# A pace for the sample's streams of keys and values in a one-core hybrid decoder step, with six stream buffers and 62 slots

## The chip, the cores and the metric

The kernel runs on one core of a Trainium2 chip. The metric is the device time of one execution in microseconds (us); the times stand in the table below.

## What is computed

One inference step of a decoder with a single layer. A prompt of 512 tokens and eight sample tokens (one each for eight requests) go through the same layer: a joint input projection, four heads of a gated linear recurrence and four heads of differential attention, an output projection, cross-attention to a memory of 256 tokens, a SwiGLU network (1024 to 2816 and back) and a last norm. Everything is float32. Each sample request attends to 4096 past tokens, whose keys and values lie in 32 pages of 128 tokens, found by a page table:

```
k_past = cache_k[l][page_table].reshape(dec_b, past_len, DA_HEADS, 2, DA_DH)
v_past = cache_v[l][page_table].reshape(dec_b, past_len, DA_HEADS, DA_DV)
attend_s = functools.partial(diff_attn_sample, k_past=k_past, v_past=v_past)
xs, s_s, k_s, v_s = run_layer(xs, pos_s, state_hgrn[l], attend_s, cache_mem_k[l], cache_mem_v[l], l)
```

A page is 256 KB, so the pages alone are 512 transfers, 134 MB.

## The kernel before

**The prompt.** Its matmuls (accumulators named mm) take float32 weights as a rounded part hi and a remainder lo, and the activations likewise, with three products for each (hi by hi, hi by lo, lo by hi). The weights are walked in one order, the plan: seven column blocks of w_in, then w_mk and w_mv (keys and values of the memory), w_out, w_mq, w_mo, and then w_gate, w_up and w_down by chunks of 512 columns. A plan row is a load of 512 KB (tile raw, three buffers); half a row is one step: ACT rounds it (hi), DVE takes the remainder (lo), and PE runs 12 matmuls with it (6 in the memory's blocks). `done["used"]` counts these steps: w_in is steps 0 to 55, the memory's 56 to 87, w_out, w_mq and w_mo 88 to 135, and the feed-forward network (FFN) starts at step 136. In matmuls of the 3072 in all, step 56 is number 672, step 88 is 864 and step 136 is 1440.

**The sample.** It multiplies the raw weights that the prompt has in SBUF anyway (`follow`: accumulators sacc, sgm, sgu, sdn). Where its data come too late for a chunk of the FFN, it loads those weights once more for itself (`s_ffn_alone` or `gate_alone`, tiles gu, dn, g of 256 KB). Its pages arrive in the stream buffers: `KBUFS` = 8 tiles of two pages (512 KB). `score_keys` (L969) takes four tiles at a time (`LUMP`), a lump of 32 small matmuls into accumulator ks, which a profile shows as 64, two for each; there are 32 such lumps. After the last one follows the sample's softmax (mxt, mxb, zt, cf, wt), then `sum_values` (L1087) with 32 lumps of eight matmuls, accumulator pv. When the values are done, the sample's output projection, its cross-attention (cs, cpv; 32 tiles cache_mem_k and cache_mem_v of 512 KB) and its own copies of w_mq and w_mo come through the same stream buffers (`load_rest`). Other tiles of 128x512 come from a pool of `SLOTS` = 59.

**The order.** The program's text doesn't set it. Each part is a generator, a stream of work; `Weave.run` (L328) builds the program by taking, again and again, the first stream by rank whose next step could start now by the `Clock`, a planner's model of the engines (L231 counts each instruction's cost). Small ranks go first; the prompt has rank 9, keys and values have rank 2 (`KRANK`, `VRANK`), loads of weights 0 and loads of pages 1. All loads are issued by SP, in the order so found, each after its buffer has come free:

```
def add(self, gen, rank, uses=""):
    self.streams.append([rank, 0.0, None, gen, uses])
    self.streams.sort(key=lambda s: s[0])
...
weave.add(score_keys(), KRANK)
...
weave.add(sum_values(), VRANK)
```

Nothing of the planner is in the program that runs; only the order that it found. L295 is the helper through which every instruction is issued, so a profile has that line for all of them, and tiles tell them apart.

Of the kernel before, what the change touches and what calls it, by code (L numbers as in the profile page):

```python
# [25 lines left out]
NB = 8  # L26
# [5 lines left out]
NCH = 8  # L32
# [1 line left out]
LAM_INIT = 0.2  # L34
LEVELS = (16, 8, 4, 2, 1)
BIG = 1e37
SLOTS = 59
SCRATCH = 4
RAW = 3
HILO = 3  # L40
KPG = 2
KBUFS = 8
LUMP = 4
NEAR, FAR = 2, 4
PBATCH = 8
LEAD = 10.0
# [2 lines left out]
KRANK = 2  # L49
# [6 lines left out]
VRANK = 2  # L56
# [64 lines left out]
    return {"consts": packed, "ropep": c["ropep"]}  # L121


TICK, FULL = 3.413, 3060
CHANGE = {
    ("wide", "narrow"): 0.18, ("narrow", "wide"): 0.16, ("exact", "wide"): 0.11, ("exact", "narrow"): 0.18,
    ("narrow", "exact"): 0.06,
# [3 lines left out]
class Clock:  # L131
# [4 lines left out]
    def __init__(self, tc):  # L136
        self.tc = tc
        self.free = dict.fromkeys(("pe", "act", "dve", "pool", "sp", "issue", "dma"), 0.0)
        self.wrote, self.used, self.rings = {}, {}, {}
        self.silu = False  # L140
        self.banks, self.freed, self.noted = {}, deque(), 0
        self.port = {"dve": deque(maxlen=24), "pool": deque(maxlen=24)}
        self.mark, self.columns = 0.0, {}
        self.form = "wide"

    def engine(self, name, nc_engine):
        return Timed(nc_engine, name, self)
# [43 lines left out]
    def _cost(self, e, op, shape, dtypes, n):  # L191
        f32r = F32R in dtypes
        if e == "pe":
            if op == "transpose":
                return 0.00105 * n
            if f32r:
                if shape[0] == 32:
                    return n * 0.000108 + 0.004
                return max(0.03, 0.000432 * n + 0.006)
            if shape[0] in (32, 64):  # L200
                return n * shape[0] / 76800 + 0.003
            return max(0.03, n / 600)
        if e == "act":
            return 0.00083 * n + (0.145 if op == "activation" else 0.04) + (0.03 if f32r else 0)
        if e == "dve":
            if op == "tensor_scalar" and n > 256:
                return 0.00052 * n + 0.067
            return 0.00105 * n + (0.125 if op == "scalar_tensor_tensor" else 0.067)
        return 0.00225 * n

    def shared(self, e, op, outs, srcs):

# [18 lines left out]
    def note(self, e, op, ins):  # L231
        i = ins.ins
        outs = [y.bass_ap for y in i.outs if hasattr(y, "bass_ap")]
        srcs = [y.bass_ap for y in i.ins if hasattr(y, "bass_ap")]
        mine = lambda aps: [a.tensor.name for a in aps if self.tc.is_my_tile(a.tensor)]
        ws, rs = mine(outs), mine(srcs)
        start = self.free[e]
        at = "dma" if op == "dma_start" else e
        for t in ws + rs:
            w, by = self.wrote.get(t, (0.0, ""))  # L240
            if by != at or at == "dma" and t in rs:
                start = max(start, w + self.LATE.get(by, 0.0))
        for t in ws if at != "dma" else ():
            start = max(start, self.used.get(t, 0.0))
        if op == "dma_start":
            start = max(start, self.free["issue"])
            self.free["issue"] = start + 0.56
            self.free[e] = start + (0.56 if e == "sp" else 0.06)
            begin = max(self.free["dma"], start + 1.1)
            a = outs[0] if ws else srcs[0]  # L250
            end = self.free["dma"] = begin + 4 * int(np.prod(a.shape)) / 0.39e6
            done = end + 0.93
            e = "dma"
        else:
            aps = outs + (srcs if e != "pe" else [])
            n = max(int(np.prod(a.shape[1:])) for a in aps)
            holds = self.shared(e, op, outs, srcs)
            if holds:
                for a, b in self.port["pool" if e == "dve" else "dve"]:
                    if a <= start < b:  # L260
                        start = b
            done = end = start + self._cost(e, op, outs[0].shape, [a.dtype for a in outs + srcs], n)
            if e == "pe":
                form = "narrow" if outs[0].shape[0] < P else "wide" if F32R in [a.dtype for a in srcs] else "exact"
                done = end = end + CHANGE.get((self.form, form), 0.0)
                self.form = form
                tick, rows = int(start / TICK), srcs[0].shape[0] / P
                if self.columns.get(tick - 1, 0) < FULL:
                    done = end = end + (end - start)
                self.columns[tick] = self.columns.get(tick, 0) + n * rows * (1 if F32R in [a.dtype for a in srcs] or op == "transpose" else 2)  # L270
            self.free[e] = end
            self.span = (start, end)
            if holds:
                self.port[e].append((start, end))
        for t in ws:
            self.wrote[t] = (done, e)
            self.mark = max(self.mark, done + self.LATE.get(e, 0.0))
        self.noted += 1
        for t in ws + rs:
            self.used[t] = max(self.used.get(t, 0.0), end)  # L280
            if t in self.banks:
                self.banks[t][1] = self.noted
# [19 lines left out]
class Weave:  # L302
# [9 lines left out]

    def add(self, gen, rank, uses=""):
        self.streams.append([rank, 0.0, None, gen, uses])
        self.streams.sort(key=lambda s: s[0])

    def _time(self, s):
        c, t = self.clock, s[1]
# [9 lines left out]
    def run(self):  # L328
        c = self.clock
        while self.streams:  # L330
            now = c.free["pe"]
            best, when = None, 0.0
            for s in self.streams:
                if s[2] is not None:
                    if not s[2]():
                        continue
                    s[2] = None
                t = self._time(s)
                if best is None or t < when:
                    best, when = s, t  # L340
                if t <= now:
                    break
            assert best is not None, "every stream waits"
            c.mark = 0.0
            try:
                y = next(best[3])
            except StopIteration:
                self.streams.remove(best)
                continue
            if y is None:  # L350
                best[1] = c.mark
            elif callable(y):
                best[1], best[2] = 0.0, y
            elif isinstance(y, tuple):
                best[1] = c.ready(y)
            else:
                best[1] = y
# [3 lines left out]
def decode_step(ctx: ExitStack, tc: tile.TileContext, io: dict):  # L361
    clock = Clock(tc)
    weave = Weave(clock)
# [560 lines left out]
    def gather(which, at, dst):  # L924

        for i, t in enumerate(dst, at):
# [5 lines left out]
                clock.free["sp"] += 0.53 + 0.03 * PBATCH  # L932
            page = pages[which][i % PBATCH]
            sync.dma_start(t, ckv[which][bass.ds(page, 1), :, :].rearrange("o p c -> (o p) c"))

    nst = NPG // KPG
    kts, vts, wts = {}, {}, [None] * 4
# [1135 lines left out]
    def sample_query(hs):  # L2073
# [10 lines left out]
        weave.add(load_keys(), 1)  # L2084
        weave.add(load_rest(), 1)
        weave.add(place_queries(), 2)
        weave.add(score_keys(), KRANK)
        yield from at_room()
        acc = att("sk")
        yield from s_gemm(hs, 2560, acc[:, :P], KT, width=P)  # L2090
# [3 lines left out]
        yield from new_scores()  # L2094
        S["sn"] = True
        yield lambda: V_FROM in raws
        weave.add(sum_values(), VRANK)
        weave.add(load_values(), 1)

    def follower():  # L2100
# [490 lines left out]
```

## Time and profile before

| | |
|---|---|
| median of 3 runs | 1152.55 us (1151.62 to 1156.77) |
| the profiled execution | 1153.06 us, span 1151.3 us |
| PE busy | 1089.1 us, 95% of the span |
| DVE, ACT, POOL busy | 545.8, 429.8, 69.0 us |
| moved by DMA | 258.80 MB, mean 225 GB/s |
| mean granted TensorE clock | 0.981 |

PE is TensorE's matmuls, PEld its weight loads, DVE VectorE, ACT ScalarE, POOL GpSimd, SP the engine that issues nearly all DMAs. A matmul's end is modelled in the profile and consecutive ones overlap, so PE's busy time is not its work; that is read from the distance of starts, or from the chain of waits, whose pieces follow each other without overlap. The granted clock 1.00 is 2.4 GHz, half of it 1.2 GHz.

### The profile page before, as it was taken

Reading aid. Unit: us, or ns where it says so; the run is one execution under the profiler, and the core shown is the slowest. Engines: PE = TensorE matmul, PEld = TensorE weight load, DVE = VectorE, ACT = ScalarE, POOL = GpSimd, SP = SyncE. Lnnn points to the kernel's source line nnn. Section 1 sums busy time; section 2 is a strip of 40 time slices with the busy share of each in tenths; the row PEclk is TensorE's granted clock in tenths of the full one; section 3 lists DMA queues with packets and bytes.
Section 4 is the critical chain, followed back from the end, with each engine's and each line's share of the span. In section 5 each row is a group of like instructions: output and inputs, shape, how many; then the busy total and the mean of one; then the engine's idle time right before and its main releaser. Section 6 shows DMA issues by size and latency. Waiting matters only on the chain.

```text
span 1151.3 us, 23340 instructions
## 1 busy us (share of the span) xinstructions
PE 1089.1 (95%) x9035; PEld 787.6 (68%) x9035; DVE 545.8 (47%) x1094; ACT 429.8 (37%) x910; POOL 69.0 (6%) x76
## 2 busy tenths in 40 slices
PE   8999989998998789999999989999999999999997
PEld 6677768776554334556655677778788787777776
DVE  6641667343557554324436355434434345444545
ACT  5411535232734564423325355433222122222333
POOL 0000032120411000000000300000000000000001
PEclk9999989998999899999999999999999999999999
DMA  7999989997997889999989832332232222234002
GB/s 263 376 362 362 369 273 328 364 374 266 302 300 274 306 312 334 364 373 377 385 328 360 330 128 57 91 91 83 83 92 78 88 64 67 64 102 126 20 1 74
DMA packets 139361, 258.80 MB, mean 225 GB/s; under 512 B 14065, under 2 KB 24305, under 8 KB 139250
## 3 DMA queue, kind: packets, MB, share of 16 engines
q1 hardware_dynamic: 138018, 256.20, 64.3%
q8 instruction: 71, 1.16, 0.4%
q10 hardware_dynamic: 1232, 1.11, 0.3%
q14 instruction: 40, 0.33, 0.1%
HBM read 248.38 MB, written 8.88 MB: 223 GB/s over the span
## 4 chain that ended last, share of the span: by engine, by line
PE 74%; DMA 16%; issue 3%; DVE 2%; ACT 2%; SPq 2%; POOL 1%; DVEq 0%; ACTq 0%; POOLq 0%
PE mm L295 53%; DMA cache_v<-cache_v 5%; PE pv L295 4%; PE ks L295 4%; DMA cache_k<-cache_k 3%; PE sdn L295 2%; PE sgu L295 2%; SPq L295 2%; DMA raw<-w_in 2%; DMA cache_mem_k<-cache_mem_k 1%; PE cs L295 1%; PE co L295 1%; PE sgm L295 1%; DMA kv<-vd 1%; ACT pr L295 1%
## 5 line engine op out<-in xcount | busy, mean ns | idle before, releaser
L295 DVE TENSOR_TENSOR lo<-raw,hi 128x512 fp32r<-128x512 f32 (+1 forms) x260 | 177.1, 683 | 428.4 <-ACT hi L295 377.2
L295 PE MATMUL mm<-sh,hi 128*128 128x512 f32 (+1 forms) x832 | 334.2, 402 | 1.4 <-ACT hi L295 1.4
L295 ACT CAST hi<-raw 128x512 fp32r<-128x512 f32 (+1 forms) x260 | 157.1, 607 | 462.0 <-PE mm L295 404.3
L295 PE MATMUL mm<-sl,hi 128*128 128x512 f32 (+1 forms) x832 | 322.7, 388 | 0.6 <-DVE sl L295 0.6
L295 PE MATMUL mm<-sh,lo 128*128 128x512 f32 (+1 forms) x832 | 322.0, 387 | 0.0
L295 PEld LDWEIGHTS mm<-sh,hi 128*128 128x128 f32 x832 | 157.1, 189 | 57.1 <-issue 23.1
L295 PEld LDWEIGHTS mm<-sh,lo 128*128 128x128 f32 x832 | 157.0, 189 | 33.2 <-DVE lo L295 0.9
L295 PEld LDWEIGHTS mm<-sl,hi 128*128 128x128 f32 x832 | 157.4, 189 | 29.4 <-DVE sl L295 1.5
L295 PE MATMUL pv<-cache_v,wt 128*32 128x512 f32 x512 | 81.9, 617 | 7.0 <-DMA cache_v<-cache_v 5.8
L295 PE MATMUL ks<-cache_k,qst 128*32 128x128 f32 x2048 | 66.8, 275 | 4.2 <-issue 2.1
L295 PEld LDWEIGHTS ks<-cache_k,qst 128*32 128x32 f32 x2048 | 55.2, 110 | 17.7 <-issue 8.4
L295 PE MATMUL mm<-hi,sh 128*128 128x512 f32 x128 | 55.8, 436 | 0.0
L295 PEld LDWEIGHTS pv<-cache_v,wt 128*32 128x32 f32 x512 | 18.3, 111 | 53.3 <-DMA cache_v<-cache_v 27.5
L295 PE MATMUL mm<-lo,sh 128*128 128x512 f32 x128 | 50.9, 398 | 0.0
L295 PE MATMUL mm<-hi,sl 128*128 128x512 f32 x128 | 50.8, 397 | 0.0
L295 DVE TENSOR_TENSOR res<-mm,res 128x512 f32<-128x512 f32 (+1 forms) x68 | 41.8, 651 | 6.8 <-PE mm L295 6.7
L295 PEld LDWEIGHTS mm<-hi,sh 128*128 128x128 f32 x128 | 24.7, 193 | 11.8 <-issue 7.8
L295 POOL TENSOR_TENSOR res<-res,par 128x512 f32<-128x512 f32 x2 | 2.3, 1144 | 483.3 <-ACT rsq L295 483.3
L295 PE MATMUL mm<-hi,mh 128*128 128x512 f32 x64 | 28.5, 445 | 0.0
L295 PEld LDWEIGHTS mm<-hi,sl 128*128 128x128 f32 x128 | 24.6, 192 | 5.7
L295 PEld LDWEIGHTS mm<-lo,sh 128*128 128x128 f32 x128 | 24.8, 194 | 4.0 <-issue 0.2
L295 PE MATMUL mm<-lo,mh 128*128 128x512 f32 x64 | 25.4, 397 | 0.2 <-DVE lo L295 0.2
(401 smaller groups left out, 1231.1 us busy)
## 6 DMA issues: line engine op xcount, KB each, us to landing
cache_k<-cache_k SPq DMA_DIRECT2D x256, 256.0 KB, 5.3
cache_v<-cache_v SPq DMA_DIRECT2D x256, 256.0 KB, 6.0
raw<-w_in SPq DMA_DIRECT2D x27, 512.0 KB, 6.0
raw<-w_down SPq DMA_DIRECT2D x22, 512.0 KB, 3.9
raw<-w_gate SPq DMA_DIRECT2D x20, 512.0 KB, 3.7
raw<-w_up SPq DMA_DIRECT2D x20, 512.0 KB, 3.7
cache_mem_k<-cache_mem_k SPq DMA_DIRECT2D x16, 512.0 KB, 10.1
cache_mem_v<-cache_mem_v SPq DMA_DIRECT2D x16, 512.0 KB, 9.7
```

Source lines behind the costliest of these rows:

```text
L295: ins = getattr(self.engine, op)(*a, **k)
```

## The change

Keys and values keep rank 2 only while they are behind a pace; ahead of it their rank is 10, after the prompt's 9. The keys' share done is held to a line from step 10 to step 62 of the prompt's weights, the values' from 60 to 136. A rank may be a function now and the streams are sorted before every choice. Two stream buffers fewer (8 to 6) and three slots more (59 to 62). The planner's model of PE gets instruction records (two for a wide matmul or a transpose, four for others) and a block of 256 of them that can't be had sooner than 5.3 us after the last one; its costs of POOL change too.

```diff
-SLOTS = 59
+SLOTS = 62
...
-KBUFS = 8
+KBUFS = 6
 LUMP = 4
+KPACE = (10, 62)
+VPACE = (60, 136)
...
-TICK, FULL = 3.413, 3060
+TICK, FULL, FETCH = 3.413, 3060, 5.3
...
-        return 0.00225 * n
+        return 0.00045 * n + 0.08 if op == "memset" else 0.0028 * n + 0.2
...
                 self.form = form
+                self.records += 2 if form == "wide" or op == "transpose" else 4
+                if self.records >= 256:
+                    self.records -= 256
+                    done = end = self.fetched = max(end, self.fetched + FETCH)
...
     def add(self, gen, rank, uses=""):
         self.streams.append([rank, 0.0, None, gen, uses])
-        self.streams.sort(key=lambda s: s[0])
+
+    @staticmethod
+    def rank(s):
+        return s[0]() if callable(s[0]) else s[0]
...
             now = c.free["pe"]
+            self.streams.sort(key=self.rank)
...
+    def pace(rank, kind, total, span):
+
+        return lambda: rank if done[kind] * (span[1] - span[0]) <= total * (done["used"] - span[0]) else 10
...
-        weave.add(score_keys(), KRANK)
+        weave.add(score_keys(), pace(KRANK, "keys", NB * nst, KPACE))
...
-        weave.add(sum_values(), VRANK)
+        weave.add(sum_values(), pace(VRANK, "values", NB * NCH, VPACE))
```

No engine gets other work, but for the sample's FFN: in the new order two of its six chunks are computed alone, with 48 loads of 256 KB more. All else is the same instructions in another order.

PE at the end of the keys. Before, the last lump of keys (ks) and the start of the sample's softmax (mxt) stand among matmuls of w_in, near matmul 570:

```order
L295 MATMUL ks_3560<-cache_k_4145,qst_535 32x128 x4
L295 MATMUL ks_3560<-cache_k_4158,qst_535 32x128 x4
L295 MATMUL mm_4074<-sh_193,hi_4219 128x512
L295 MATMUL mm_4074<-sl_194,hi_4219 128x512
L295 MATMUL mm_4074<-sh_193,lo_4224 128x512
L295 MATMUL mm_3959<-sh_210,hi_4296 128x512
L295 MATMUL mm_3959<-sl_211,hi_4296 128x512
L295 MATMUL mm_3959<-sh_210,lo_4301 128x512
L295 MATMUL mxt_4409<-con,mx_4396 1x128
```

In the changed kernel the same place on PE lies among the prompt's attention (sc are its scores, oda its sums of values) and the matmuls of the memory's weights:

```order
L301 MATMUL ks_4087<-cache_k_4984,qst_529 32x128 x4
L301 MATMUL ks_4087<-cache_k_4987,qst_529 32x128 x4
L301 MATMUL sc_5192<-kT_3444,qT_4678 128x384
L301 MATMUL sc_5193<-kT_3444,qT_4678 128x384
L301 MATMUL mxt_5227<-con,mx_5221 1x128
L301 MATMUL oda_5234<-pr_5082,vda_2450 128x128
L301 MATMUL oda_5234<-pr_5082,vda_2470 128x128
L301 MATMUL mm_4936<-hi_5063,mh_4137 128x512
L301 MATMUL mm_4936<-lo_5075,mh_4137 128x512
```

The last lump of keys has moved from the prompt's w_in into its attention. By matmul 576 all 32 lumps of keys stood on PE before, and 22 do now; by matmul 1152 all 32 lumps of values stood there, and 22 do now; the last lump of values went from matmul 1044 to 1416.

SP where the loads of the FFN's weights begin. Before, they follow each other, with the sample's own copies of one gate chunk (g) among them:

```order
L295 DMA raw_8322<-w_mo 128x2x512
L295 DMA raw_8324<-w_gate 128x2x512
L295 DMA raw_8337<-w_gate 128x2x512
L295 DMA raw_8417<-w_gate 128x2x512
L295 DMA raw_8451<-w_gate 128x2x512
L295 DMA raw_8556<-w_up 128x2x512
L295 DMA raw_8624<-w_up 128x2x512
L295 DMA g_8689<-w_gate 128x512
```

Now the sample's w_out and w_mq stand between them on SP:

```order
L301 DMA cache_v_8471<-cache_v 128x512
L301 DMA w_out_8476<-w_out 128x1024
L301 DMA w_out_8481<-w_out 128x1024
L301 DMA raw_8502<-w_gate 128x2x512
L301 DMA w_out_8522<-w_out 128x1024
L301 DMA w_out_8524<-w_out 128x1024
L301 DMA w_mq_8526<-w_mq 128x1024
L301 DMA w_mq_8531<-w_mq 128x1024
L301 DMA raw_8552<-w_gate 128x2x512
L301 DMA raw_8659<-w_up 128x2x512
```

The sample's output projection and cross-attention, with their loads, have moved behind the start of the FFN.

## Rows read from the trace of the kernel before

**Rows 1.** The profile page: PE's busy time, and the clock, DMA share and rate in 40 slices

```profile
PE 1089.1 (95%) x9035; PEld 787.6 (68%) x9035; DVE 545.8 (47%) x1094; ACT 429.8 (37%) x910; POOL 69.0 (6%) x76
...
PEclk9999989998999899999999999999999999999999
DMA  7999989997997889999989832332232222234002
GB/s 263 376 362 362 369 273 328 364 374 266 302 300 274 306 312 334 364 373 377 385 328 360 330 128 57 91 91 83 83 92 78 88 64 67 64 102 126 20 1 74
```

**Rows 2.** The chain that ended last, from the page, by engine

```profile
PE 74%; DMA 16%; issue 3%; DVE 2%; ACT 2%; SPq 2%; POOL 1%; DVEq 0%; ACTq 0%; POOLq 0%
```

**Rows 3.** Windows: stretch, length, busy us by engine (instructions), clock, DMA share, GB/s

```profile
0.00:286.80 286.80, 262.89 (x4103) 206.96 (x4104) 146.40 (x318) 102.05 (x227) 33.04 (x45) 0.97 0.95 334
286.80:611.50 324.70, 299.88 (x1749) 166.25 (x1748) 148.88 (x337) 143.39 (x326) 19.90 (x16) 0.97 0.94 334
611.50:729.90 118.40, 114.15 (x755) 85.27 (x754) 60.52 (x128) 55.46 (x131) 10.76 (x9) 1.00 0.56 197
729.90:1140.80 410.90, 409.74 (x2422) 327.23 (x2421) 183.44 (x301) 127.11 (x223) 3.02 (x4) 1.00 0.24 71
```

**Rows 4.** The same windows, matmuls of the prompt's weights (tile mm) on PE alone

```profile
0.00:286.80 286.80, 152.23 (x576) 0.97 0.95 334
286.80:611.50 324.70, 152.81 (x577) 0.97 0.94 334
611.50:729.90 118.40, 70.16 (x290) 1.00 0.56 197
729.90:1140.80 410.90, 368.81 (x1633) 1.00 0.24 71
```

**Rows 5.** The chain in order of time: start, us, what; one piece of each kind

```profile
168.84 1.88 PE ks L295 x64
...
527.83 1.85 PE pv L295 x16
...
566.36 1.86 PE sgm L295 x32
...
761.82 21.98 PE mm L295 x96
```

**Rows 6.** Windows of 50 us in which the DMA engines are full

```profile
50.00:100.00 50.00, 48.27 (x708) 38.41 (x710) 23.33 (x45) 14.40 (x25) 0.00 (x0) 1.00 1.02 363
...
500.00:550.00 50.00, 48.98 (x265) 30.77 (x264) 15.66 (x26) 14.29 (x27) 0.52 (x1) 1.00 1.04 380
```

**Rows 7.** Groups of PE by line: busy us, mean ns, idle before

```profile
L295 PE MATMUL cs<-cache_mem_k,qx 128*32 128x256 f32 x128 | 10.0, 390 | 1.3 <-DMA cache_mem_k<-cache_mem_k 1.3
...
L295 PE MATMUL cpv<-cache_mem_v,w 128*32 128x512 f32 x64 | 8.9, 600 | 0.5 <-DMA cache_mem_v<-cache_mem_v 0.5
```

**Rows 8.** DMA issues: tile, queue, count, KB each, median us from issue to landing

```profile
cache_k<-cache_k SPq DMA_DIRECT2D x256, 256.0 KB, 5.3
cache_v<-cache_v SPq DMA_DIRECT2D x256, 256.0 KB, 6.0
...
g<-w_gate SPq DMA_DIRECT2D x8, 256.0 KB, 5.1
```

**Rows 9.** Waits of PE: who for whom, us in total, times, longest

```profile
PE pv L295 <- DMA cache_v<-cache_v: 5.8, 3, 2.4
PE pd L295 <- issue: 5.5, 4, 3.4
PE so L295 <- issue: 5.0, 1, 5.0
```

**Rows 10.** Timeline of PE, where it waited longest for its own instructions

```profile
277.48 1.41 PE L295 MATMUL so<-st,qm 128*32 128x128 f32 x8 [4.97 <-issue]
278.82 0.80 PE L295 MATMUL mm<-sh,hi 128*128 128x512 f32 x1
279.42 0.63 PE L295 MATMUL mm<-sl,hi 128*128 128x512 f32 x1
```

More of the change, by code (lines that the diff above doesn't have):

```diff
@@ L143, in __init__ @@
         self.mark, self.columns = 0.0, {}
-        self.form = "wide"
+        self.form, self.records, self.fetched = "wide", 0, 0.0
     def engine(self, name, nc_engine):
```

## The prediction

> **What bounds the kernel now.** I read the page first, then windows cut where the prompt's matmuls reach round counts, then the chain.
>
> On the page PE is busy for 95% of the span [rows 1], which says little, since its busy time overlaps and stretches. The line below it says more: the DMA engines are full for the first 22 slices or so, at up to 385 GB/s, and run at two or three tenths from slice 24 on. The chain is DMA for 16% of the span [rows 2], some 184 us, so PE does wait for loads, and it must be in the first part.
>
> The windows show where [rows 3]. They are cut where the prompt has done 576, 1152 and 1440 of its 3072 matmuls, which the counts of mm confirm, one or two at an edge counted twice [rows 4]; matmul 1440 is the start of the FFN. In the first two windows the DMA share is 0.95 and 0.94, PE is idle for 23.9 and 24.8 us, and the granted clock is 0.97; between its two levels of 2.4 and 1.2 GHz a mean of 0.97 costs 3% of the time, 8.6 and 9.7 us. In the FFN, window 4, PE is idle for 1.2 us in 410.9, at a clock of 1.00 and a DMA share of 0.24.
>
> How much is lost there comes from the work. The prompt's matmuls take 21.98/96 = 0.229 us each where they run undisturbed, a lump of keys 1.88, one of values 1.85, and 32 records of the sample's projections (sgm) 1.86 [rows 5]. Window 1: 576 x 0.229 + 32 x 1.88 = 192 us, which leaves 95 of 286.8. Window 2: 131.9 + 32 x 1.85 = 191, which leaves 134 of 324.7. Window 3: 288 x 0.229 = 66, which leaves 52 of 118.4. In what is left lie the other matmuls (recurrence, attention, cross-attention and the sample's); counted by kind and taken at the spacing of their nearest kind in the chain they come to about 41, 55 and 50 us, an estimate that may be off by 5 in each. So PE loses about **54, 79 and 2 us** in the three windows: 135 us that aren't work. Idle time and half clock explain 67 of the first two; the rest are changes between kinds and matmuls that wait with their operands half there.
>
> The loads bound it from the other side. Full, the DMA engines move 363 to 380 GB/s [rows 6]; I take 375. What stands on SP up to the last load that a matmul of a window reads is 90, 111, 24 and 30 MB, so 240, 296, 63 and 81 us. Against work of 233, 246, 116 and about 400 us, windows 1 and 2 are bound by loads, 3 and 4 by PE, and loads can't be taken forward from window 2 into 4.
>
> **The change, part by part.** *The pace.* By the new order the loads that the same four stretches need are 70, 95, 27 and 76 MB, of which 49 MB fall into the first 384 matmuls of the FFN. At 375 GB/s these are 187, 254, 71 and 201 us (131 in those 384). PE's work becomes:
>
> Stretch 1: 131.9 + 22 x 1.88 + 41 = 214 us, now above its loads (187). The loss doesn't vanish, as start-up, changes of kind and the recurrence's chains stay; I take two thirds of 54, so 36, between 20 (the load waits and all half clock gone) and 54 (nothing gained). 214 + 36 = **250**, before 286.8.
>
> Stretch 2: 131.9 + 10 x 1.88 + 22 x 1.85 + 40 = 231 us, below its loads of 254: this one stays bound by DMA, since the memory's steps are half as long on PE (6 matmuls) while the values' pace counts steps. Before, window 2 lasted 29 us more than its loads; the same on top gives **283**, before 324.7. Bounds: 254, the loads alone, and 231 x 324.7/246 = 305, PE losing the same share as before.
>
> Stretch 3: 66 + 10 x 1.85 + 29 + 3 = **117**, before 118.4. The last ten lumps of values come in; the sample's cross-attention and projections go out.
>
> Stretch 4: what went out comes back here: cs 10.0 and cpv 8.9 us [rows 7], five groups of sgm at 1.86 [rows 5] and some 2 of small ones, 30 us; a gate chunk of the sample of 2 us comes too. The 131 us of loads in the first 384 matmuls stand against 126 of work, and I add 8 for waits there: 410.9 + 40 = **451**. Bounds 443 and 470, the latter if those loads overrun as window 1 did (286.8/240).
>
> *Two chunks alone* cost 48 x 256 KB = 12.6 MB more (such loads: [rows 8]), contained in the 49 MB. Their matmuls replace those of two chunks that followed the prompt, at about the same work. *Sorting, the costs of POOL, a rank that is a function* are work of the planner only and leave no instruction; what orders they cause is counted above. *Three slots more* are room for the loads of the chunks alone; nothing in the trace names a wait for a slot, so 0, covered by PE being the bound in the FFN.
>
> *Six buffers.* The trace has no run with six. A lump holds four tiles until PE takes it, so two can be filled ahead instead of four. Bounds: 0, if lumps come no faster than loads refill, and 2.8 us a lump (two tiles, 1.05 MB at 375) if PE is there first, so 179 us over 64 lumps. I take 0, nearest to the rows: with eight, PE's own waits for values sum up to 5.8 us [rows 9], and in stretch 1 a lump comes every 250/22 = 11.4 us instead of every 7 or so, while four tiles take 5.6 us.
>
> *The blocks of instruction records.* PE does wait for its own instructions: 4.97 us before one group, after which matmuls run at 0.43 to 0.6 us apart [rows 10], and 10.5 us in the two longest entries [rows 9]. A plan that avoids this could win 0 to 13 us; the small matmuls of the recurrence stand in the same bursts as before, so I take 0. The Trainium skill (Runtime: NRT & Kernel Launch, section Instruction fetch mechanics) says that crossing a block of 256 instructions is mostly hidden; by it this part is worth 0 as well, while rows 10 show a wait that was not hidden, so if all of them went the sum would be 1100 instead of 1113.
>
> Sum: 250 + 283 + 117 + 451 + 12.3 (the rest of the span and what lies around it, 1153.06 - 1140.8, unchanged) = **1113 us**, 40 below. The profiled execution took 1153.06 and the median is 1152.55, so the sum holds for both.
>
> The rate matters for stretch 2 alone. A row of 50 us shows 380 GB/s [rows 6]. The Trainium skill (DMA: Bandwidth & Descriptors, section Where 436 GB/s comes from) puts the limit of a core's loads from HBM at about 358; by that stretch 2 would need 266 us of loads and the sum would be 1125. The measured row decides.
>
> **Rivals.** *More is won*: with loads off the path in stretch 1 and half off in stretch 2, only changes of kind are lost: 234 + 261 + 117 + 443 + 12 = about 1070. For it: window 4 loses next to nothing. Against it: the prompt's attention and recurrence have chains of their own through ACT and DVE, in which PE waits with few matmuls at hand. Up to 1095 I give it 0.15.
>
> *It is given back in the FFN*: the 49 MB stand on SP among the gate's and up's weights, the prompt's rows wait in the same queue behind them, and the stretch that was free of waits gets 30 us of them (131 x 1.19 less 126), while stretch 1 keeps its 54. 1113 + 18 + 22 = 1153. For it: SP issues in order, and a load that waits for a stream buffer holds up all behind it. Against it: PE had idle DMA to spare there, a share of 0.24. 0.17 for 1135 to 1158.
>
> *Slower: the six buffers starve the lumps.* PE reaches a lump before its last two tiles have landed. With the sum's gain of 40 us the point is 40/64 = 0.6 us a lump; at 0.9 us a lump it is 1113 + 58 = 1171. For it: from issue to landing a page takes 5.3 to 6.0 us at the median [rows 8], and stretch 2 has its loads at the limit. Against it: the slower beat of lumps, as above. 0.08.
>
> *The pace does nothing on the chip*: excluded as far as the order shows, since the lumps do stand elsewhere.
>
> **How the numbers follow.** The forecast's own case, 1095 to 1135, gets 0.58; more is won 0.15; given back 0.17; slower 0.08; 0.02 for anything beyond. The range that leaves out no more than 2 in 10 is 1083 to 1150, which cuts half of the first rival, the upper third of the second and the third whole. Half a percent, about what a measurement can tell from no change, is 1146.8 to 1158.3. Below it lie the forecast, the first rival and half of the second, 0.82; inside 0.10; above 0.08.
>
> **What would show it.** Right: in the new trace matmul 576 is reached near 250 us, 1152 near 533, 1440 near 650; the DMA share falls to about 0.75 in stretch 1 and stays above 0.9 in stretch 2; the DMA rate in the first 100 us of the FFN rises from below 100 [rows 1] to over 300 GB/s; chain DMA falls below 10%. Wrong: PE waits for cache_k or cache_v by far more than 6 us (six buffers), PE's waits for weights in the FFN (given back), or matmul 576 still near 287 us, which would mean that loads never bounded stretch 1.

## The result and the profile after

| | before | changed |
|---|---|---|
| median, 8 runs each, on one chip | 1153.7 us | 1159.3 us |
| profiled execution, span | 1153.06, 1151.3 us | 1158.22, 1156.5 us |
| ratio, 95% interval | | 1.0052 [1.0027, 1.0076] |

The change made the kernel slower by half a percent; 1113 us, 40 less than before, was forecast. The same four stretches, cut where the prompt has done 576, 1152 and 1440 matmuls, are now these (length, then busy us of PE, PEld, DVE, ACT and POOL with their instructions, clock, DMA share, GB/s); the second fence has mm on PE alone, to show the cuts:

```profile
0.00:264.60 264.60, 239.56 (x3454) 187.22 (x3455) 143.31 (x306) 98.29 (x216) 31.80 (x45) 0.97 0.82 277
264.60:575.00 310.40, 280.73 (x1981) 174.69 (x1980) 143.43 (x324) 143.35 (x325) 17.36 (x13) 0.95 0.90 305
575.00:688.90 113.90, 113.58 (x641) 81.80 (x640) 58.71 (x109) 52.28 (x122) 11.36 (x10) 1.00 0.73 251
688.90:1146.00 457.10, 453.73 (x2826) 335.17 (x2825) 194.64 (x345) 131.90 (x244) 3.66 (x6) 1.00 0.46 159
```

```profile
0.00:264.60 264.60, 151.43 (x576) 107.17 (x577) 6.22 (x10) 8.25 (x12) 0.97 0.82 277
264.60:575.00 310.40, 150.16 (x577) 105.58 (x576) 8.48 (x14) 8.28 (x12) 0.95 0.90 305
```

Against [rows 3] the stretches are 22.2, 14.3 and 4.5 us shorter and the FFN is 46.2 longer. The loads did spread as planned: the DMA share of stretch 1 went from 0.95 to 0.82, and the FFN moves 159 GB/s, not 71. But PE's idle time, length less busy, is 25.0 and 29.7 us in stretches 1 and 2, where it was 23.9 and 24.8, and the clock of stretch 2 fell from 0.97 to 0.95: a mean of 0.95 costs 15.5 us there, 9.7 before. The page of the changed kernel says the same in its slices, against [rows 1] and [rows 2]:

```profile
PE 1090.1 (94%) x8909; PEld 780.7 (68%) x8909; DVE 546.7 (47%) x1094; ACT 427.6 (37%) x910; POOL 66.4 (6%) x76
...
PEclk8999999989888899999999999999999999999999
DMA  7899967878888699999976687999852221233102
GB/s 248 299 325 312 312 223 263 274 264 261 261 252 307 193 339 342 372 337 342 324 264 208 203 309 290 357 360 377 290 163 85 82 82 56 65 108 110 56 1 73
...
PE 71%; DMA 19%; DVE 4%; SPq 2%; ACT 1%; issue 1%; DVEq 0%; ACTq 0%
```

DMA has a larger share of the chain, 19% for 16%, while its engines are less full in stretches 1 and 2. The chain of stretch 2 alone, by line, tells which loads. First the kernel before, from 286.8 to 611.5 us:

```profile
by line: PE mm L295 29.6%; DMA cache_v<-cache_v 16.3%; PE pv L295 14.3%; DMA cache_mem_k<-cache_mem_k 5.2%; DMA kv<-vd 3.3%; ACT pr L295 3.0%; SPq L295 3.0%; PE oda L295 3.0%; DMA raw<-w_mk 2.6%; PE sc L295 2.2%; PE sgm L295 2.1%; DMA raw<-
```

The changed kernel, from 264.6 to 575 us, and two of the longest pieces of that chain:

```profile
by line: PE mm L301 31.2%; DMA cache_k<-cache_k 18.6%; PE pv L301 14.3%; DMA raw<-w_mk 6.6%; DMA kv<-vd 3.4%; PE ks L301 3.3%; SPq L301 3.0%; PE oda L301 2.8%; DMA raw<-w_out 2.5%; PE ss L301 2.2%; DMA cache_v<-cache_v 1.6%; PE pt L301 1.2%
...
310.69 13.52 DMA cache_k<-cache_k
333.59 12.90 DMA raw<-w_mk
```

The wait for values went (16.3 to 1.6%) and a wait for keys of about the same size came (18.6%). PE's and SP's entries in the list of waits name it (us in total, times, longest):

```profile
PE ks L301 <- DMA cache_k<-cache_k: 19.3, 16, 6.3
PE so L301 <- DVE st L301: 6.5, 1, 6.5
PE zt L301 <- DVE z L301: 4.4, 1, 4.4
PE pd L301 <- issue: 4.0, 2, 3.5
...
SPq L301 <- PE ks L301: 62.0, 28, 7.2
SPq L301 <- PE pv L301: 25.6, 24, 4.4
```

SP now stands 62.0 us at pages whose buffer PE still holds; before it was 12.8 us, as the list of the kernel before has it:

```profile
SPq L295 <- PE ks L295: 12.8, 14, 3.7
```

Nor do pages land much sooner now that fewer bytes are under way: 5.0 us for a page of keys, 5.3 before, and 5.1 for one of values, 6.0 before [rows 8]. The DMA issues of the changed kernel (tile, queue, count, KB each, median us to landing):

```profile
cache_k<-cache_k SPq DMA_DIRECT2D x256, 256.0 KB, 5.0
cache_v<-cache_v SPq DMA_DIRECT2D x256, 256.0 KB, 5.1
...
kv<-vd SPq DMA_DIRECT2D x8, 256.0 KB, 10.7
```

### The profile page after: what moved, and what is told of

Same layout as the page of the kernel before. It is cut to its first block, busy times and chain, and to the rows that moved or that the text cites. A ratio compares the mean times of both kernels' runs of the same rounds, so it can differ in the third digit from the quotient of the medians.

```text
span 1156.5 us, 23161 instructions
## 1 busy us (share of the span) xinstructions
PE 1090.1 (94%) x8909; PEld 780.7 (68%) x8909; DVE 546.7 (47%) x1094; ACT 427.6 (37%) x910; POOL 66.4 (6%) x76
## 4 chain that ended last, share of the span: by engine, by line
PE 71%; DMA 19%; DVE 4%; SPq 2%; ACT 1%; issue 1%; DVEq 0%; ACTq 0%
PE mm L301 49%; DMA cache_k<-cache_k 6%; PE pv L301 5%; PE ks L301 3%; DMA raw<-w_in 3%; SPq L301 2%; DMA raw<-w_mk 2%; DMA kv<-vd 2%; PE cs L301 2%; PE sdn L301 2%; PE sgu L301 2%; DMA gu<-w_up 1%; PE co L301 1%; DVE lo L301 1%; PE sgm L301 1%
## 5 line engine op out<-in xcount | busy, mean ns | idle before, releaser
L301 PE MATMUL mm<-sh,hi 128*128 128x512 f32 (+1 forms) x832 | 337.9, 406 | 0.9 <-ACT hi L301 0.9
L301 PE MATMUL ks<-cache_k,qst 128*32 128x128 f32 x2048 | 76.2, 285 | 19.4 <-DMA cache_k<-cache_k 19.3
L301 PEld LDWEIGHTS ks<-cache_k,qst 128*32 128x32 f32 x2048 | 58.1, 113 | 40.6 <-DMA cache_k<-cache_k 32.4
L301 PE MATMUL pv<-cache_v,wt 128*32 128x512 f32 x512 | 71.0, 599 | 0.0
L301 PE MATMUL mm<-hi,sh 128*128 128x512 f32 x128 | 55.1, 431 | 0.0
L301 PEld LDWEIGHTS pv<-cache_v,wt 128*32 128x32 f32 x512 | 16.3, 109 | 36.8 <-issue 20.7
L301 POOL TENSOR_TENSOR res<-sh,sl 128x512 f32<-128x512 f32 x8 | 10.6, 1349 | 275.7 <-PE cpt L301 267.7
```

What stands on the lines that cost most here:

```text
L301: ins = getattr(self.engine, op)(*a, **k)
```

## The experiments

Three questions: are stretches 1 and 2 bound by loads; which part of the change does what; and how far does the order alone, with no part of the change, move the time. Lengths of the stretches are of the profiled runs, which can lie some us off the median (e6's took 1143.2 us, its median is 1149.5); ratios have 95% intervals against the kernel before on the same chip.

### Half of the pages' bytes

d1_before_half has the order of before on PE (of 9035 records 26 stand a place or two off), but each page's transfer brings the first half of its columns, and PE reads that half twice; d2_after_half is the same on the changed kernel. The planner still counts whole pages.

```diff
-            sync.dma_start(t, ckv[which][bass.ds(page, 1), :, :].rearrange("o p c -> (o p) c"))
+            clock.planned = 2
+            sync.dma_start(t[:, :256], ckv[which][bass.ds(page, 1), :, :].rearrange("o p c -> (o p) c")[:, :256])
+            clock.planned = 1
```

> The kernel before in its own order, each page loaded by its first half alone (256 of 512 columns, so 67 MB instead of 134) and that half read twice by the matmuls; the planner is told the full size, so that no instruction moves. Theory L (what the prediction held: the rate of the loads bounds the first two stretches): matmul 576 before 255 us instead of 286.8, matmul 1152 before 530 instead of 611.5, 1060 to 1090 us in all. Theory W (PE loses some 50 and 75 us there to waits that the order sets, latencies and chains, whatever the loads' rate): both marks within 20 us of the kernel before's, 1130 to 1150 us.

> The change in its own order with half pages in the same way. Theory L: little to win, since the loads are spread by the pace: 1130 to 1155 us, stretch 1 at 255 to 265 us. Theory W in its form for the change (six buffers let loads be issued only when PE has taken a lump, so each waits for the time of a landing): the waits of PE for cache_k shrink from 19 us to 5 to 10, as a lump then needs half the time to land, 1125 to 1145 us.

d1 took 1113.5 us, 0.9665 [0.9629, 0.9701], and d2 1124.6, 0.9761 [0.9724, 0.9799], two runs each. Neither theory's range holds either time. d1 lies between them, with matmul 576 where theory W had it and matmul 1152 40 us ahead of before; d2 lies just below both, and PE's wait for keys went from 19.3 to 12.0 us where theory W asked for 5 to 10. The first two stretches of d1, and then of d2:

```profile
0.00:267.00 267.00, 253.66 (x4102) 202.21 (x4103) 146.55 (x318) 102.06 (x227) 33.29 (x45) 0.99 0.74 226
267.00:571.30 304.30, 286.19 (x1749) 162.96 (x1748) 149.02 (x337) 143.60 (x326) 19.93 (x16) 0.97 0.79 252
```

```profile
0.00:253.00 253.00, 235.81 (x3454) 185.83 (x3455) 145.08 (x306) 98.08 (x217) 33.53 (x45) 0.98 0.64 197
253.00:543.60 290.60, 267.98 (x1981) 172.43 (x1980) 143.19 (x324) 142.51 (x325) 17.41 (x13) 0.95 0.70 210
```

Rate times length gives the bytes: stretch 1 of before moved 334 x 286.8 = 95.8 MB and 60.3 in d1, stretch 2 108.4 and 76.7. The shorter packets are slower by the byte (summed over the trace's packets of stretch 1, 360 GB/s at 2 KB before and 304 at 1 KB in d1), so the engines' own time, share times length, is the fairer measure: 272 us became 198 in stretch 1 and 305 became 240 in stretch 2. Both are now below PE's work of 233 and 246 us, and yet each stretch got only **20 us** shorter. In the same order, with the same work on PE, 40 of the 133 us lost there hang on the pages' bytes; the other 93 did not go with them. Loads are still waited for in d1's stretch 2, by the chain's lines:

```profile
by line: PE mm L296 33.8%; PE pv L296 16.0%; DMA cache_v<-cache_v 6.7%; DMA cache_mem_k<-cache_mem_k 5.4%; ACT pr L296 3.8%; SPq L296 3.7%; PE oda L296 3.0%; DMA kv<-vd 2.7%; DMA mt<-memT 2.5%; issue 2.4%; PE sc L296 2.3%; PE sgm L296 2.3%;
```

The four loads in it make 17.3%, 53 us, at engines that are 0.79 full: that speaks for single landings that PE comes to too early rather than for a rate, though the loads that were not halved cannot be told apart in it.

Where the rest of PE's time goes can be counted. The prediction set the loads beside a PE work of 233 and 246 us, in which everything but the prompt's matmuls and the lumps was an estimate (41 and 55). In the table each PE record counts from its start to the next start, less the idle time between, summed by kind; idle is length less busy, and the other kinds are what remains (us).

| stretch, kernel | length | idle | prompt's matmuls | lumps | other kinds |
|---|---|---|---|---|---|
| 1, in the prediction | | | 131.9 | 60.2 | 41 |
| 1, before | 286.8 | 23.9 | 148.2 | 62.9 | 51.8 |
| 1, d1 | 267.0 | 13.3 | 144.7 | 60.0 | 49.0 |
| 1, changed | 264.6 | 25.0 | 147.0 | 43.3 | 49.3 |
| 2, in the prediction | | | 131.9 | 59.2 | 55 |
| 2, before | 324.7 | 24.8 | 147.2 | 78.4 | 74.3 |
| 2, d1 | 304.3 | 18.1 | 146.3 | 66.7 | 73.2 |
| 2, changed | 310.4 | 29.7 | 145.7 | 79.9 | 55.1 |

A time from start to start can hide a wait, and the half clock is in them (8.6 and 9.7 us before), so these are upper bounds of the work. Without the idle time PE is taken for 263 and 300 us before and still for 254 and 286 in d1. Of the 40 us that halving took off, 17 were idle time and 15 the lumps; the prompt's matmuls and the other kinds lost 8 us and stay 53 above the prediction's figures.

On the changed kernel the same halving gives 11.6 and 19.8 us: the pace took 8 us of the pages' price off stretch 1 and none off stretch 2.

### The parts, singly and together

Between before and the changed kernel lie three parts: the pace, the buffers (six with 62 slots, or eight with 59), and the planner's new costs (records and POOL). All eight combinations of them ran.

```diff
-SLOTS = 62
+SLOTS = 59
-KBUFS = 6
+KBUFS = 8
```

This turns the changed kernel into e1_pace_8buf, and stands in e3, e5 and e8 too; its reverse on the kernel before is e7_before_6buf.

```diff
-        weave.add(score_keys(), pace(KRANK, "keys", NB * nst, KPACE))
+        weave.add(score_keys(), KRANK)
...
-        weave.add(sum_values(), pace(VRANK, "values", NB * NCH, VPACE))
+        weave.add(sum_values(), VRANK)
```

Both lines make e2_nopace_6buf, with eight buffers e3_nopace_8buf; the second line alone with eight buffers makes e5_kpace_8buf, in which the keys alone have a pace.

```diff
-        return 0.00045 * n + 0.08 if op == "memset" else 0.0028 * n + 0.2
+        return 0.00225 * n
...
-                self.records += 2 if form == "wide" or op == "transpose" else 4
-                if self.records >= 256:
-                    self.records -= 256
-                    done = end = self.fetched = max(end, self.fetched + FETCH)
```

This puts the old costs back: e6_after_oldcosts, and with eight buffers e8_pace_8buf_old. e9_after_norec drops the records alone and keeps the new costs of POOL.

> The change with eight stream buffers and 59 slots again; pace and planner costs stay. Theory A (six buffers starve the lumps of keys: SP waits 62 us for PE's ks, and the loads behind it on SP wait too): the waits of PE for cache_k fall from 19 us to under 8, SP's waits for ks from 62 to under 25, matmul 576 is reached near 250 us instead of 264.6 and matmul 1152 near 540 instead of 575; about 1125 us (1110 to 1140). Theory B (the order itself: what is won before the FFN comes back in it, and keys among the prompt's attention cost as much as they win): 1150 to 1162 us, waits of PE for cache_k still above 12 us. Theory C (the planner's blocks of records make a worse order): about as the change, 1155 to 1162.

> The change without the pace (both ranks 2 again), six buffers and 62 slots stay. Theory A: slower than the change, as the keys are asked for as fast as they come with two tiles in reserve: 1170 to 1190 us, SP's waits for ks above 60 us. Theory B: about the kernel before, 1148 to 1158 us. Theory C: 1155 to 1162 us.

> No pace, eight buffers, 59 slots: of the change only the planner's costs (records, POOL) are left. Theories A and B: as the kernel before within 0.5%, 1148 to 1158 us. Theory C: slower than the kernel before by 5 us or more, 1159 us and up.

> Eight buffers, 59 slots, the keys held to their pace, the values at rank 2 as before. Theory A: the keys' part of the gain, some 30 us before the FFN, and only some of the sample's rest in the FFN: 1115 to 1135 us. Theory B: what comes back in the FFN is less than in the change (24 loads alone instead of 56), but the gain before it is small too: 1145 to 1158 us.

> The change without the planner's new costs (records, POOL): pace, six buffers and 62 slots stay. Without pace and with eight buffers these costs alone made 1163.7 us from 1154. If they cost 9 us in every order (theory C): 1146 to 1153 us. If that was an accident of one order: 1154 to 1163 us.

> The kernel before with six buffers and 62 slots alone. Theory A (six buffers starve): 1160 to 1185 us. Theory W (what is late in one place isn't in another): 1148 to 1160 us. If the costs always add 9 us and the same edit with them ran in 1155 us: 1146 us.

> The pace alone: eight buffers, 59 slots and the planner's old costs. It completes the eight combinations of pace, buffers and costs. Theory A (buffers decide): clearly under the same with six buffers, which ran in 1149.5: 1120 to 1140 us. Theory W (PE's losses in the first two stretches are set by order and latency, not by buffers): 1145 to 1158 us.

> The change without the blocks of instruction records; the new costs of POOL stay. If the records are what costs the 10 us between the change (1159) and the change with the old costs (1149.5): 1147 to 1153 us, with the wait of PE for its own instructions no longer than in the change (4.0 us). If POOL's costs do it: 1156 to 1162. If neither does and it is the accident of the order: anything between.

| kernel | pace | buffers | costs | ratio to before | stretches 1, 2, 3, FFN |
|---|---|---|---|---|---|
| before | none | 8 | old | 1 (1153.7 us) | 287, 325, 118, 411 |
| e7 | none | 6 | old | 1.0231 [1.0203, 1.0260] | 292, 318, 151, 407 |
| e3 | none | 8 | new | 1.0089 [1.0054, 1.0124] | 313, 316, 113, 412 |
| e2 | none | 6 | new | 1.0000 [0.9968, 1.0033] | 285, 296, 146, 417 |
| e5 | keys | 8 | new | 1.0031 [1.0006, 1.0055] | 274, 319, 148, 407 |
| e8 | both | 8 | old | 1.0097 [1.0075, 1.0119] | 275, 307, 115, 454 |
| e1 | both | 8 | new | 1.0045 [1.0021, 1.0068] | 271, 305, 115, 454 |
| e6 | both | 6 | old | 0.9962 [0.9939, 0.9985] | 259, 299, 117, 456 |
| e9 | both | 6 | POOL alone | 0.9970 [0.9950, 0.9990] | 265, 302, 115, 460 |
| changed | both | 6 | new | 1.0052 [1.0027, 1.0076] | 265, 310, 114, 457 |

*Beside the pace six buffers do not starve the lumps.* With eight (e1), PE's wait for keys fell from 19.3 to 8.8 us and SP's for PE from 62.0 to 26.6, and the time stayed: another wait, SP for the values' lumps, rose from 25.6 to 34.8. The three entries in e1:

```profile
PE ks L301 <- DMA cache_k<-cache_k: 8.8, 21, 1.9
...
SPq L301 <- PE pv L301: 34.8, 17, 13.0
SPq L301 <- PE ks L301: 26.6, 14, 6.9
```

p2 below, another order of the changed kernel, has 8.0 us of PE's wait for keys instead of 19.3 and is no faster. Without the pace it is less clear: in e7 PE's waits for keys and values are 18.7 us, before 7.7, and the 1160 to 1185 us expected of starving came (1180.1); in e2 they are 23.6 us, and the time is that of before.

*No part has a worth of its own.* By the medians six buffers are worth +27 us without pace at old costs (e7 against before) and -17 with it (e6 against e8); at new costs they are worth -9 (e2 against e3) and +1 (the changed kernel against e1). The pace is worth +12 with eight buffers at old costs (e8) and -31 with six (e6 against e7). The new costs are worth +9 (e3 against before), -25 (e2 against e7), -8 (e1 against e8) and +10 (the changed kernel against e6).

*The stretches show more than the sums.* With the pace stretch 1 is 259 to 275 us, without it 285 to 313. With both paces the FFN is 454 to 460, otherwise 407 to 417.

*The waits for instructions are not the records model's to remove.* They stand as issue in the list of PE's waits. One entry has another cause: so, 5.0 us before [rows 9], waits for the recurrence's state st, and in all nine such waits of over 1 us in these kernels PE goes on 0.10 us after DVE's first st ends. Without so the entries add up to 8.4 us before, 13.3 in e3, which has the new costs and no pace, 4.0 in the changed kernel and 2.5 in e6, which has no records. Seven orders without the pace have 4.4 to 13.3 us, eleven with it 2.5 to 5.8, whatever the costs.

*Against the expectations.* That the buffers decide was to give 1110 to 1140 us in e1, 1170 to 1190 in e2, 1115 to 1135 in e5 and 1120 to 1140 in e8; none came. That the new costs lose 9 us in every order fits e3 and e6, but not e2 beside e7. e9 came in the range for the records (1150.5), though its waits of kind issue are 5.3 us even without so, where no more than 4.0 were expected.

### Two more edits of the fastest kernel

k1_old_kv is e6 with the planner told that the tile kv of the recurrence (the broadcast of vd, 10.7 us to landing) lands 7 us later; k2_old_v112 is e6 with the values' pace ending at step 112.

```diff
+        n = dst.tensor.name
+        clock.wrote[n] = (clock.wrote[n][0] + 7.0, "dma")
+        clock.mark = max(clock.mark, clock.wrote[n][0])
```

```diff
-VPACE = (60, 136)
+VPACE = (60, 112)
```

> The change with the old costs, and the planner told that a row of the sample's recurrence (kv, which lands 10 us after its issue, where the planner reckons with under 3) comes 7 us later. Theory W: the waits of ACT for kv (37.5 us in the change), of DVE behind it (20.6) and of PE behind that (6.5 to 9.9) fall to a third, and the second stretch is 10 to 20 us shorter: 1128 to 1142 us. Theory L (rate of loads): no change, 1146 to 1153.

> The change with the old costs and the values' pace ending at step 112 instead of 136: the sample's rest starts some 24 steps earlier, one chunk of the FFN less is computed alone (32 loads instead of 56). If what the FFN gives back is due to how much of the sample lies in it: matmul 1440 some 12 us later, the FFN 15 to 25 us shorter than the 456 it took, 1135 to 1146 us. If the time only moves from one side of step 136 to the other: 1146 to 1154 us.

k1 gave 1152.0 us, 0.9976 [0.9954, 0.9999], and k2 1152.8, 0.9981 [0.9957, 1.0005]: neither helps. k1 did what it was made for, since ACT's waits for kv fell from 38.8 us in e6 to 6.8 and DVE's behind them from 19.0 to 5.5; so these waits were not what the time hung on. In k2 the FFN is 424 us, 31 shorter than in e6, and the stretch before it 156, 38 longer. The sample's cross-attention is not cheaper ahead of matmul 1440 than behind it.

### The same kernels in another order

A part that is worth +27 beside one part and -17 beside another may be no part's worth at all. Each of these kernels has one planner's cost moved by 0.01 us, which makes another order and means nothing on the chip.

```diff
-    ("wide", "narrow"): 0.18, ("narrow", "wide"): 0.16, ("exact", "wide"): 0.11, ("exact", "narrow"): 0.18,
+    ("wide", "narrow"): 0.19, ("narrow", "wide"): 0.16, ("exact", "wide"): 0.11, ("exact", "narrow"): 0.18,
```

p1 is before with it, p2 the changed kernel, p3 is e6, p4 is e8; p5 and p6 are before with 0.17 and 0.20.

> The kernel before with one of the planner's costs, that of a change from wide to narrow matmuls, at 0.19 us for 0.18: no part of the change, and no meaning for the chip beyond another order. Theory A (the parts decide by what they do): within 3 us of the kernel before, 0.997 to 1.003. Theory B (the order that the planner happens to find decides, and orders scatter): 5 us or more off in either direction is as likely as not; over the four kernels of this call at least two are over 5 us from their twins.

> The changed kernel with the same cost at 0.19. Theory A: 1156 to 1162, so 1.002 to 1.008 of the kernel before, as the changed kernel. Theory B: anywhere from 1145 to 1175; the sign against the kernel before may turn.

> The changed kernel with the planner's old costs (1149.5, the fastest so far) with the same cost at 0.19. Theory A: 1146 to 1153, 0.993 to 0.999. Theory B: nearer to the middle of the orders, 1150 to 1165, as the fastest of several was picked by chance.

> The pace alone with eight buffers, 59 slots and the old costs (1166.3, slower by 1%) with the same cost at 0.19. Theory A: 1163 to 1170, 1.007 to 1.013. Theory B: nearer to the middle, 1150 to 1163, as the slow one was a chance as well.

> The kernel before with the cost of a change from wide to narrow matmuls at 0.17 us for 0.18. Theory B (orders scatter) with before as a lucky order: 1160 to 1180, so 1.005 to 1.02. Theory B with before as an ordinary order and 0.19 as a bad one: 1148 to 1160, 0.995 to 1.005.

> The kernel before with the same cost at 0.20. Before as a lucky order: 1160 to 1180, 1.005 to 1.02. Before as an ordinary one: 1148 to 1160, 0.995 to 1.005.

| kernel | its twin | ratio to before | stretches 1, 2, 3, FFN |
|---|---|---|---|
| p1 | before, 1 | 1.0138 [1.0088, 1.0188] | 308, 327, 115, 411 |
| p5 | before, 1 | 0.9996 [0.9969, 1.0024] | 299, 316, 114, 410 |
| p6 | before, 1 | 1.0061 [1.0037, 1.0084] | 305, 318, 114, 412 |
| p2 | changed, 1.0052 | 1.0062 [1.0032, 1.0092] | 259, 311, 118, 456 |
| p3 | e6, 0.9962 | 0.9930 [0.9906, 0.9954] | 261, 301, 117, 456 |
| p4 | e8, 1.0097 | 1.0044 [1.0023, 1.0065] | 274, 304, 115, 455 |

0.01 us in a table moved the kernel before by 1.4%, more than the whole change did. The first expectation had asked for two of four kernels more than 5 us from their twins; p1 is 16 and p4 8 off, p2 and p3 are not. p5 (1153.2 us) fits before as an ordinary order, p6 (1160.1) before as a lucky one. So orders scatter: four orders of before lie 17 us apart, the pairs with pace and six buffers 2 and 4, though a pair is too few to tell a spread. The windows of p1 show where its 16 us are, 21 more in stretch 1, with a clock of 0.95 and a DMA share no fuller than before:

```profile
0.00:307.60 307.60, 276.01 (x4191) 214.99 (x4192) 149.68 (x331) 105.27 (x235) 31.70 (x45) 0.95 0.95 331
307.60:634.40 326.80, 297.91 (x1743) 164.41 (x1742) 142.97 (x333) 141.20 (x321) 19.67 (x16) 0.96 0.95 338
634.40:749.00 114.60, 109.64 (x705) 86.17 (x705) 61.44 (x117) 55.74 (x130) 10.66 (x9) 0.97 0.45 151
749.00:1160.00 411.00, 409.77 (x2422) 327.24 (x2421) 183.45 (x300) 127.14 (x223) 3.04 (x4) 1.00 0.23 71
```

p3 is the fastest kernel of all, **1145.6 us, 0.9930 [0.9906, 0.9954]**: the pace, six buffers and 62 slots with the planner's old costs. It beats both kernels, though it is the best of eighteen and was picked after the fact:

```profile
0.00:260.90 260.90, 237.35 (x3454) 186.71 (x3454) 142.53 (x306) 98.07 (x216) 31.70 (x45) 0.97 0.83 280
260.90:562.00 301.10, 280.55 (x1965) 179.57 (x1964) 145.09 (x325) 144.23 (x326) 18.08 (x13) 0.94 0.89 308
562.00:678.90 116.90, 116.90 (x658) 82.62 (x657) 58.07 (x108) 51.77 (x121) 11.34 (x10) 1.00 0.77 264
678.90:1135.20 456.30, 453.07 (x2827) 334.93 (x2826) 194.88 (x345) 131.72 (x244) 3.73 (x6) 1.00 0.46 159
```

Read by families: four orders of before have a mean ratio of 1.005, two of the changed kernel 1.0057, and three without records (e6, e9, p3) 0.9954. So against the one order of before the change loses half a percent, against the family it is even, and without the records model it wins 1%, as far as so few orders tell; with eight buffers (e8 and p4) it does not. The 10 us of the records lie in stretch 2: 310 and 311 us with them, 299, 302 and 301 without. PE is idle there for 29.7 us in the changed kernel and for 20.5 in p3. Which of the moved instructions makes those 10 us was not tried.

## Why the prediction was wrong

**The step that failed** is "windows 1 and 2 are bound by loads". It set a DMA share of 0.95 and 90 and 111 MB at 375 GB/s beside PE's work, and as the loads were the longer it took PE's loss for theirs. Halving the pages' bytes gives back 40 us of 133. The other side of the comparison was too small: with half the bytes PE's time without idle is still 254 and 286 us, not 233 and 246, so that in stretch 1 it is longer than the loads' 240 and in stretch 2 nearly as long as their 296. What was taken for lost to loads was in good part PE's own time, in changes between kinds and in the other kinds' matmuls. That a queue is full says that loads are issued as early as they can be, not that PE would be sooner with fewer.

*Stretch 1.* 250 was forecast, 264.6 came. Of the 22.2 us won 19.6 are the ten lumps that moved out (62.9 to 43.3 us); nothing else moved by more than 2.5. Of the loss of 54 us two thirds were to stay; 264.6 - 214 = 51 stayed, which is nearly the bound at which nothing is won. The loss that d1 takes out with the bytes is 20, which would have been the term to start from, and the pace does less than halving does.

*Stretch 2.* 283 was forecast, 310.4 came, beyond the upper bound of 305; this is the largest miss, 27 of the 45 us. The bytes were right: 305 x 310.4 = 94.7 MB for 95. They were not the bound, as with 34 MB less d2 still takes 290.6. The loss here was 79 and is 310.4 - 231 = 79: only the moved work left, 19 us of other kinds by the table, and 5 of it came back as idle time. The wait for values became one for keys, and the ten last lumps of keys now stand among the prompt's attention.

*Stretch 3.* 117 forecast, 113.9 came: right, with the last ten lumps of values in it.

*The FFN.* 451 forecast, 457.1 came, 46.2 us more than before where 40 were added. The moved work came as counted: cs, cpv and sgm take 26.9 us from start to start and the small ones 2.3, for 30. The sample's own FFN matmuls (sgu, sdn) take 5.6 more, for 2. The 8 us for waits did not come, as PE is idle for 3.4 us, 2.2 more than before. Its first 101 us move 331 GB/s, as foreseen, with PE busy for 99.29 of 101.10:

```profile
688.90:790.00 101.10, 99.29 (x675) 60.24 (x674) 41.54 (x93) 31.23 (x61) 0.63 (x2) 1.00 0.88 331
```

In their place stands a term that the sum did not have. The prompt's 1632 matmuls take 376.2 us there for 366.6, at a clock of 1.00 in both, because the sample's work cuts them into 79 runs instead of 32. PE's timeline shows the price: from start to start a matmul takes 0.23 us, the last one before another kind 0.31 and the first one after it 0.34.

```profile
706.46 0.39 PE L301 MATMUL mm<-sl,hi 128*128 128x512 f32 x1
706.69 0.39 PE L301 MATMUL mm<-sh,lo 128*128 128x512 f32 x1
707.00 1.93 PE L301 MATMUL sgm<-w_mq,h1s 128*32 128x256 f32 x32
708.87 0.50 PE L301 MATMUL mm<-sh,hi 128*128 128x512 f32 x1
709.21 0.40 PE L301 MATMUL mm<-sl,hi 128*128 128x512 f32 x1
709.44 0.39 PE L301 MATMUL mm<-sh,lo 128*128 128x512 f32 x1
```

At 0.19 us a run the same price explains some 25 of the 133 us lost in stretches 1 and 2 before, which have 58 and 72 such runs.

*The sum.* The four misses, 14.6 + 27.4 - 3.1 + 6.1, are the 45 us between 1113 and 1158.2. So the mechanism was half of it: work moves out of the full stretches at its price and comes back in the FFN at its price and that of the changes of kind. The other half, that PE's loss goes with the load on the DMA engines, is what did not come.

*The other terms.* Six buffers at 0: right as to starving, since eight win nothing beside the pace (e1). Without the pace they cost 27 us in one order (e7), where stretch 3 alone is 32 us longer, and won 9 in another (e2). *The records* at 0, within 0 to 13 us of gain: beside the pace and six buffers they cost some 10, and a bound on the losing side was missing. The 4.97 us of [rows 10] were misread there: they end with a row of the recurrence that lands late. In the kernel before's timeline ACT waits for kv, DVE's st for ACT, and PE goes on at 277.48 us, 0.10 us after the first of the four st has ended:

```profile
276.54 1.28 ACT L295 ACTIVATE kv<-kv,skT 128x128 f32<-128x128 f32 x4 [6.51 <-DMA kv<-vd]
277.03 1.17 DVE L295 SCALAR_TENSOR_TENSOR st<-st,scols,kv 128x128 f32<-128x128 f32 x4 [6.02 <-ACT kv L295]
```

The 3.4 us of pd [rows 9] do end with a block of instructions, as the last section tells.

*The rate*: the Trainium skill (DMA: Bandwidth & Descriptors, section Where 436 GB/s comes from) puts a core's loads from HBM at about 358 GB/s. A slice of 29 us in the changed kernel's page has 377, so the trace is above it again. Neither figure set a stretch, since stretch 2 ran at 305.

*The rivals.* "Given back in the FFN" gave 1153 with stretch 1 keeping its 54, and that half came; its 30 us of waits in the FFN did not. "Six buffers" had its sign in the trace, 19.3 us of waits for keys, and e1 and p2 show that the sign isn't the cause. None said that the one order before was a good one of its family: 1.0138 and 1.0061 for two of three siblings.

## What to carry to other kernels

Before a plan that spreads loads, run the same order with half the bytes: a DMA share of 0.95 beside an idle PE is no proof that the bytes bind, and here halving the largest share of them gave back less than a third of the loss. Count the engine's own time from its starts, changes of kind included, before calling the rest a loss. Work that moves from a full stretch into a free one costs its full price there, so such a move can win only what the loads themselves cost. Where a planner sets the order, time three or four orders of the kernel before (a cost shifted by next to nothing) ahead of judging a part: here they lie 1.4% apart, and a single pair would have given each part either sign.

## What was not expected of the hardware

*A full queue is not a full rate.* Stretch 2 of the changed kernel has a DMA share of 0.90 at 305 GB/s, the first 101 us of its FFN 0.88 at 331. Packets differ: summed over the trace's packet records, those of 512 bytes moved 119 GB/s in that stretch and those of 2 KB 354, while those of 4 KB moved 394 in these 101 us. The broadcast of vd to kv takes 10.7 us to land for 256 KB, a page of 256 KB takes 5.0.

*What issue is.* Where PE stood still for 1 us or more under this name, other than ahead of so, a packet of 16384 bytes on the queue of instructions had ended 0.96 to 1.63 us before PE went on, in all 42 cases of the kept traces.

*Landings hardly got shorter.* A page of keys lands in 5.3 us before (one of values in 6.0) and in 5.0 (5.1) with the share of stretch 1 down from 0.95 to 0.82, and single pieces of the chain still are 13.52 us long.

*The pace did not raise the clock.* The mean granted clock of stretch 2 was 0.95 in the changed kernel and 0.94 in p3, below the 0.97 of before. Between 1.2 and 2.4 GHz that is 16 to 18 us where it was 10; what PE did less of there was not tried apart. In stretch 1 it stayed at 0.97, and with half the bytes (d1) it was 0.99.
